# Two edits to the order of side work in a two-layer hybrid decoder kernel: a pause of the weight-sum jobs begins earlier, and two sigmoids wait for the last split of attention

## The chip, the cores and the metric

The kernel runs on one core of a Trainium2 chip. The core has a matrix engine (TensorE, PE in the profile, with PEld for its weight loads), a vector engine (VectorE, DVE), an engine for activation functions (ScalarE, ACT), a general engine (GpSimd, POOL) and a sync engine (SyncE, SP) that here only issues DMAs. Each engine works through its own queue of instructions in order; an instruction that waits for a semaphore holds up everything behind it on that engine. DMAs are issued from the queues of SP, ACT and POOL and then run by themselves.

The metric is the device time in microseconds (us) of one execution. The time of the kernel is the median over its runs.

## The reference

What is computed is a decoder trunk of two layers on 512 tokens of width 1024, all in fp32:

```python
def hybrid_layer(x, g_mix, w_in, sinks, w_a, w_b, w_out, g_mlp, w_up, w_down):
    h = rmsnorm(x, g_mix)
    z = h @ w_in
    aq, ak, av, rq, rk, rv, rg, ga, gb = jnp.split(z, SPLIT_POINTS, axis=-1)
...
    ya = sliding_window_sink_attention(aq, ak, av, sinks) @ w_a
...
    r = chunkwise_retention(rq, rk, rv)
    r = r * lax.rsqrt(jnp.mean(r * r, axis=-1, keepdims=True) + EPS)
    r = r.reshape(B, S, RET_V) * jax.nn.silu(rg.astype(jnp.float32))
    yb = r.astype(x.dtype) @ w_b
    mixed = jax.nn.sigmoid(ga) * ya + jax.nn.sigmoid(gb) * yb
    x = x + mixed @ w_out
    h2 = rmsnorm(x, g_mlp)
    x = x + jnp.square(jax.nn.relu(h2 @ w_up)) @ w_down
    return x
```

The attention looks back over 128 tokens, has 8 query heads of width 64 and a learned sink per head; the retention has 4 heads with values of width 256; the MLP is 4096 wide. A final RMS norm follows the second layer.

## The kernel before

**Precision.** Every fp32 product is made of three matmuls on rounded parts: each operand is split into a high part (a copy to the type float32r, on ACT) and a low part (the remainder, on DVE), and high times high, high times low and low times high are added in PSUM. So each block of weights that arrives from DRAM (tile `raw`, 128 partitions by 1024 numbers) costs one ACT copy (`hi`, line 342) and one DVE subtraction (`lo`, line 343) before PE may use it. Up to four blocks are split ahead of use. The same split is applied to activations by `split` (lines 417 and 418 without a scale, 420 and 421 with one).

**Fewer multiplications.** The products with the value weights, four of the retention gates, the output weights `w_wo` and the MLP weights are done in a Strassen-like form on 2 by 2 blocks with seven products instead of eight. That form needs sums of weight blocks. Where two sums share an earlier one, that earlier sum is prepared in DRAM by pairs of DMAs on POOL's queue: a plain copy of a block (line 231), and a DMA that adds a second block to it (line 234). The generator `sum_steps` (lines 216 to 245) lists these jobs for a layer, in the order of their need. For layer 0 it has one more pair at its end, for the last MLP block: a copy to `sums_last` (line 242), then two adding DMAs to it (lines 244 and 245), each of which must wait until the DMA before it has landed.

**When a job is issued.** `pace(src)` (lines 252 to 262) is called from many places where an engine has just written a tile `src`. At each second call it puts a tiny copy `mark` of one column of `src` on POOL (line 259), so that POOL waits for that tile, and behind it one step of the generator. While `quiet[0]` is true a call does nothing and isn't counted. The calls of a layer come in this order: 8 in attention, 8 from the gates of attention, 2 from the first retention query and key; then quiet; 8 from the values; 4 from the other queries and keys and 16 from the two retention pairs; 8 from the retention gates `gb`; the mixing `put_mixed` of 8 chunks; and 4 from the first half of the output product. There are none in the MLP.

**The end of the mixing stage.** x, the running activation, stays in SBUF, but from the gates of attention on its tile holds the mixed values; the true x is loaded again from DRAM. `put_mixed(c)` multiplies chunk c with its gate, adds it to `mixed[c]` (which is `x[:, c, :]`), and after odd chunks calls `first` or `second` of `Mixed`, which build the blocks for the output product; `third(0)` and `third(2)` follow after the last chunk. `third(0)` uses chunks 0, 1, 4 and 5, `third(2)` the chunks 2, 3, 6 and 7; both end in splits at lines 417 and 418. Then lines 1306 and 1307 load x again, in eight DMAs on POOL's queue, each of which may start when the splits of its chunk are done. `output()` (line 1335) multiplies with `w_wo` in seven pairs of blocks (matmuls at line 1351; each block has 24 of them) and adds the results to the reloaded x (lines 1373 and 1374).

**The end of attention.** Attention is a background task that is advanced between the chunks of the input projection. For each of four blocks of tokens, `weighted(n)` (line 753) takes its results from PSUM (lines 767 and 768) and splits them (line 769, by 417 and 418); the split of the last block is kept as `last_split`. The projection with `w_a` (lines 1189 to 1199) starts from these splits. Around it lie the sigmoid of the attention gates (line 1178), the four products `silu(i)`, i = 0 to 3, which turn the retention gates rg into rg times its sigmoid (line 1062 on ACT, 1063 on DVE), the last query and key of `qk(1)` (rotated at lines 638 to 644), and `turned.build`, which prepares blocks of the normed input for the last four retention gates (`last_gates`, matmuls at line 1015, tile `rg` in PSUM).

**What sets the order.** The framework's scheduler gives each engine its queue: it takes instructions by the order of the program, but lets a later one go ahead when by its own model of the times an earlier one is not ready. `tc.issue_after(ins)` adds an edge of order alone: what is issued in its block stands behind `ins` in the queue of the engine of `ins`. Other engines are not bound by it.

## Time and profile before

| What | Value |
|---|---|
| median of 3 runs | 1474.15 us |
| lowest and highest run | 1473.31 and 1476.63 us |
| the profiled execution | 1475.95 us |
| its span, first to last instruction | 1473.9 us |
| its mean granted TensorE clock | 0.997 |
| DMA traffic | 302.83 MB, 205 GB/s on the mean |
| DMAs from POOL's queue | 129.78 MB |

The profile was taken from one execution. Its times are microseconds from the start of the span. A row of the timeline shows start, duration, engine, line of the code, operation, the tile written and the tiles read, how many instructions are merged, and in brackets how long the engine was idle before and what ended that wait. A row of windows shows a stretch of time, then for each engine its busy time with the number of instructions, and then the granted clock of TensorE as a share of full speed, the busy share of the DMA engines and GB/s. A row of waits reads: who, for whom, total us, times, longest. The chain of waits is followed back from the last instruction, each step to what released it.

### The profile page before, as it was taken

The page shows a single profiled execution, that of the slowest core. Times are in us where ns is not written, and L with a number is a line of the kernel's source. Part 1 is how long each engine was busy: PE and PEld are TensorE (multiplying, and loading weights), DVE is VectorE, ACT ScalarE, POOL GpSimd, SP SyncE. Part 2 cuts the span into 40 slices and gives each one's busy share as a digit, 9 for nine tenths or more (in the row PEclk, how much of TensorE's full clock was granted, in tenths as well). Part 3 has the DMA queues.
Part 4 walks back from the last instruction along what each step waited for, and adds up shares of the span by engine and source line. Part 5 has one row for each costly group of instructions (what it writes and reads, how often), then busy time and mean ns, then how long its engine had stood idle before and what let it go on. Part 6 is the DMA issues. An engine that isn't in the chain of part 4 may idle for free.

```text
span 1473.9 us, 22472 instructions
## 1 busy us (share of the span) xinstructions
PE 1451.4 (98%) x8185; PEld 1271.8 (86%) x8185; DVE 1181.1 (80%) x1776; ACT 974.5 (66%) x1590; POOL 229.7 (16%) x335
## 2 busy tenths in 40 slices
PE   9999999999899999999999999999999999999998
PEld 7888888888888999999888888888889889999997
DVE  6977877868698888888779788878689888888885
ACT  6656655544487777787656576556447877777775
POOL 0011002321101111111200110022211111111120
PEclk9999999999999999999999999999999999999999
DMA  7598249999735766666964983499975477777664
GB/s 258 180 292 235 90 141 301 285 281 263 201 113 186 182 176 178 180 182 184 313 195 150 288 260 104 151 306 259 280 187 185 154 196 194 191 195 190 175 187 149
DMA packets 97295, 302.83 MB, mean 205 GB/s; under 512 B 11425, under 2 KB 11553, under 8 KB 90785
## 3 DMA queue, kind: packets, MB, share of 16 engines
q0 software_dynamic: 36512, 129.78, 37.5%
q1 hardware_dynamic: 59952, 170.32, 33.9%
q8 instruction: 64, 1.05, 0.3%
q10 hardware_dynamic: 720, 1.31, 0.2%
q14 instruction: 47, 0.38, 0.1%
HBM read 261.78 MB, written 120.06 MB: 259 GB/s over the span
## 4 chain that ended last, share of the span: by engine, by line
PE 90%; DMA 3%; issue 3%; DVE 2%; ACT 1%; POOL 1%; DVEq 0%; POOLq 0%; ACTq 0%
PE mm L395 21%; PE mm L396 21%; PE mm L394 21%; PE wo L1351 4%; PE rg L1015 3%; PE b L394 3%; PE b L395 3%; PE b L396 3%; PE rv L395 2%; PE rv L394 2%; PE rv L396 2%; PE mm L410 2%; DMA sums_up<-w_pair_in 1%; PE score L780 1%; PE pT L745 1%
## 5 line engine op out<-in xcount | busy, mean ns | idle before, releaser
L342 ACT ACTIVATE hi<-raw 128x1024 fp32r<-128x1024 f32 (+1 forms) x393 | 400.1, 1022 | 255.1 <-PE mm L395 120.0
L343 DVE TENSOR_TENSOR lo<-raw,hi 128x1024 fp32r<-128x1024 f32 (+1 forms) x394 | 458.9, 1174 | 93.7 <-ACT hi L342 90.7
L394 PE MATMUL mm<-xh,hi 128*128 128x512 f32 (+1 forms) x912 | 319.1, 354 | 1.7 <-DVE rot L642 0.6
L395 PE MATMUL mm<-xl,hi 128*128 128x512 f32 (+1 forms) x912 | 319.6, 353 | 0.0
L396 PE MATMUL mm<-xh,lo 128*128 128x512 f32 (+1 forms) x912 | 316.2, 353 | 0.1
L394 PEld LDWEIGHTS mm<-xh,hi 128*128 128x128 f32 x912 | 173.2, 190 | 25.7 <-ACT xh L420 1.3
L395 PEld LDWEIGHTS mm<-xl,hi 128*128 128x128 f32 x912 | 173.3, 190 | 21.9
L396 PEld LDWEIGHTS mm<-xh,lo 128*128 128x128 f32 x912 | 172.2, 190 | 21.5 <-DVE lo L343 0.3
L395 PE MATMUL mm<-r,hi 128*128 128x256 f32 (+1 forms) x608 | 189.3, 311 | 0.5 <-DVE r L418 0.5
L394 PE MATMUL mm<-r,hi 128*128 128x256 f32 (+1 forms) x608 | 186.2, 312 | 3.4 <-ACT r L417 2.9
L396 PE MATMUL mm<-r,lo 128*128 128x256 f32 (+1 forms) x608 | 189.0, 311 | 0.0
L394 PEld LDWEIGHTS mm<-r,hi 128*128 128x128 f32 x608 | 115.5, 190 | 12.8 <-ACT r L417 4.0
L395 PEld LDWEIGHTS mm<-r,hi 128*128 128x128 f32 x608 | 115.8, 190 | 9.4 <-DVE r L418 1.4
L396 PEld LDWEIGHTS mm<-r,lo 128*128 128x128 f32 x608 | 115.8, 190 | 6.3
L1674 POOL DMA_DIRECT2D y<-eu x56 | 63.0, 1401 | 372.0 <-DVE eu L1659 371.9
L395 PE MATMUL mm<-lo,r 128*128 128x512 f32 (+1 forms) x276 | 104.3, 387 | 0.0
L396 PE MATMUL mm<-hi,r 128*128 128x512 f32 (+1 forms) x276 | 100.9, 387 | 0.0
L394 PE MATMUL mm<-hi,r 128*128 128x512 f32 (+1 forms) x276 | 98.3, 389 | 0.3 <-ACT r L417 0.2
L394 PE MATMUL b<-hi,r 128*128 128x512 f32 x180 | 70.6, 392 | 1.9 <-DVE eu L1659 1.9
L1351 PE MATMUL wo<-r,hi 128*128 128x256 f32 x384 | 71.0, 287 | 0.0
L283 DVE TENSOR_TENSOR raw<-raw 128x512 f32<-128x512 f32 x56 | 38.5, 687 | 40.5 <-DMA raw<-w_pair_in 32.4
L395 PE MATMUL b<-lo,r 128*128 128x512 f32 x180 | 70.2, 390 | 0.0
(337 smaller groups left out, 2873.0 us busy)
## 6 DMA issues: line engine op xcount, KB each, us to landing
raw<-w_in_in SPq DMA_DIRECT2D x65, 512.0 KB, 5.5
sums_down<-w_down_in POOLq DMA_DIRECT2D x30, 1024.0 KB, 12.8
sums_up<-w_pair_in POOLq DMA_DIRECT2D x56, 512.0 KB, 12.1
raw<-w_down_in SPq DMA_DIRECT2D x45, 512.0 KB, 7.4
raw<-w_pair_in SPq DMA_DIRECT2D x84, 256.0 KB, 3.7
y<-y POOLq DMA_DIRECT2D x62, 256.0 KB, 9.7
y<-eu POOLq DMA_DIRECT2D x61, 256.0 KB, 8.5
raw<-sums_down SPq DMA_DIRECT2D x30, 512.0 KB, 7.2
```

Source lines behind the costliest of these rows:

```text
L283: nc.vector.tensor_tensor(raws[i][:, at], last[:, LEFT], last[:, RIGHT], ALU.add)
L342: state["high"] = nc.scalar.activation(hi[:, at], raw[:, at], AF.Copy).ins
L343: nc.vector.tensor_tensor(lo[:, at], raw[:, at], f32(hi[:, at]), ALU.subtract)
L394: nc.tensor.matmul(ps, ah, bh, start=start and i == 0, stop=False, **more)
L395: nc.tensor.matmul(ps, ah, bl, start=False, stop=False, **more)
L396: latest[0] = nc.tensor.matmul(ps, al, bh, start=False, stop=stop and i == n - 1, **more).ins
L410: latest[0] = nc.tensor.matmul(ps, w[:, cols(j, c)], moving[k][low], start=first, stop=bool(final)).ins
L745: nc.tensor.transpose(pt[:, i * P : (i + 1) * P], sm[:, at : at + P], ident)
L780: nc.tensor.matmul(ps[:, g * w : (g + 1) * w], q_s[g][:, c, at], part[:, keys], start=i == 0, stop=i == 1)
L1015: nc.tensor.matmul(o, w[:, cols], v, start=start and k == 0 and n == 0 and w is hi and v is vh, stop=k == 3 and n == 1 and w is lo, skip_g ...
L1351: latest[0] = nc.tensor.matmul(o, w[:, cols], v, start=start and first and n % 2 == 0 and w is hi and v is vh, stop=final and w is lo, ski ...
L1674: nc.gpsimd.dma_start(y[:, 2 * j + m, i * T : (i + 1) * T], t, **how)
```

## The change

Two places in `layer_body` change, and both hold for either layer.

```diff
         with tc.issue_after(last_exp[0]):
             for hs in (slice(0, T // 2), slice(T // 2, T)):
                 nc.scalar.activation(x[:, :, hs], x[:, :, hs], AF.Sigmoid)
-            for i in range(4):
+            for i in range(2):
+                silu(i)
+        with tc.issue_after(last_split[0]), tc.issue_after(last_split[1]):
+            for i in range(2, 4):
                 silu(i)
...
         group("w_b", layer, rT, [put_mixed(c) for c in range(4)], {1: second_pair})
+        quiet[0] = True
         for c in range(6, KD):
             gate_tile(c)
             chunk("w_in", layer, xs, gate(gates[c]))
         for c in range(4, KD):
-            quiet[0] = c > 5
             chunk("w_b", layer, rT, put_mixed(c))
         quiet[0] = False
```

The first edit: `silu(2)` and `silu(3)`, so far bound to stand behind the last exponential of attention on ACT, now stand behind the last split of attention, on ACT (the two sigmoids) and on DVE (the two products).

The second edit: the pause, which held for the calls of `put_mixed(6)` and `put_mixed(7)`, now also covers those of gates 6 and 7 and of `put_mixed(4)` and `put_mixed(5)`: four calls of `pace` per layer that no longer count. `quiet[0]` is set back to false at the same place as before, which in the program stands ahead of `third` and of the eight reloads of x; the next calls are those of `output()`.

## The prediction

> **What bounds the kernel.** I read the page first, then the waits of PE, the chain of waits, windows around the largest hole, and the queues that lead into it.

> ```profile
> span 1473.9 us, 22472 instructions
> PE 1451.4 (98%) x8185; PEld 1271.8 (86%) x8185; DVE 1181.1 (80%) x1776; ACT 974.5 (66%) x1590; POOL 229.7 (16%) x335
> PE wo L1351 <- DVE lo L343: 7.0, 1, 7.0
> PE mm L394 <- ACT r L417: 3.0, 3, 1.7
> ```

> PE is busy for 98% of the span, so time can come almost only from its holes: 1473.9 - 1451.4 = 22.5 us in all. The largest single wait, 7.0 us, is in the output product (L1351) of layer 0; the next row, at three places, is for ACT's split of activations (L417). The change touches the surroundings of both.

> ```profile
> 366.75:387.30 20.55, 20.55 (x171) 20.34 (x169) 13.21 (x17) 12.31 (x17) 5.16 (x8) 1.00 0.78 170
> 387.30:394.35 7.05, 0.00 (x1) 0.00 (x0) 1.88 (x3) 0.00 (x0) 0.00 (x0) 0.84 0.67 223
> 394.35:398.57 4.22, 4.22 (x19) 4.22 (x20) 4.22 (x6) 1.37 (x2) 1.07 (x2) 0.50 0.47 133
> ...
> 370.69 10.45 DMA sums_last<-sums_down
> 383.77 8.62 DMA x<-xT_in
> 393.08 1.23 DVE lo L343
> 394.35 14.54 PE wo L1351 x104
> ```

> The windows show PE without work for 7.05 us (387.30 to 394.35) and then 4.22 us at a granted clock of 0.50. The last four rows are the chain of waits: an adding DMA to `sums_last`, the reload of x, a weight split on DVE, PE. So a job of the weight sums, which nothing needs before the last MLP block, stands ahead of the reload that the output product needs. POOL's queue in both layers shows how:

> ```profile
> 360.02 0.83 POOL L234 DMA_DIRECT2D sums_down<-w_down_in  x1 [4.53 <-DMA sums_down<-w_down_in]
> 360.56 0.60 POOL L259 COPY mark<-gb 128x1 f32<-128x1 f32 x1
> 370.69 1.08 POOL L244 DMA_DIRECT2D sums_last<-sums_down  x1 [9.53 <-issue]
> 381.48 0.83 POOL L245 DMA_DIRECT2D sums_last<-w_down_in  x1 [9.72 <-DMA sums_last<-sums_down]
> 382.12 3.44 POOL L1307 DMA_DIRECT2D x<-xT_in  x6
> 395.28 1.07 POOL L1307 DMA_DIRECT2D x<-xT_in  x2 [9.71 <-DVE r L418]
> ...
> 1078.68 0.51 POOL L259 COPY mark<-m 128x1 f32<-128x1 f32 x1 [0.99 <-DVE m L1275]
> 1103.39 1.16 POOL L1307 DMA_DIRECT2D x<-spill  x2 [14.67 <-DVE r L418]
> 1120.17 1.06 POOL L1307 DMA_DIRECT2D x<-spill  x2 [0.58 <-DVE r L418]
> ```

> In layer 0 POOL waits 9.53 us before L244 and 9.72 us before L245; six reloads follow at once at 382.12. In layer 1 no job stands there: its last mark is at 1078.68, the reloads wait only for DVE's splits, and PE has no hole there.

> DVE's queue in layer 0:

> ```profile
> 366.79 0.68 DVE L418 TENSOR_TENSOR late<-x,late 128x512 fp32r<-128x512 f32 x1
> 378.35 1.29 DVE L418 TENSOR_TENSOR r<-x,r 128x512 fp32r<-128x512 f32 x2
> 392.47 0.69 DVE L1373 TENSOR_TENSOR x<-x,kept 128x512 f32<-128x512 f32 x1 [11.70 <-DMA x<-xT_in]
> 394.21 0.69 DVE L418 TENSOR_TENSOR r<-x,r 128x512 fp32r<-128x512 f32 x1
> ```

> DVE reaches L1373 at 380.77 (392.47 - 11.70) and stands until x lands. Behind it in the queue are the weight splits that PE lacks from 387.30 on, 6.5 us later, and the last split of `third(2)` (394.21), for which the last two reloads wait.

> **The change, part by part: the pause.** First, which jobs it moves. `pace` marks by window:

> ```profile
> 0.00:737.00 737.00, 17.44 (x29) 1.00 0.74 211
> 737.00:1473.90 736.90, 16.62 (x27) 1.00 0.70 200
> ```

> Layer 0 uses 29 steps of its generator, layer 1 27. By the order of the calls 56 have counted when the four chunks of the first mixing group are done: 28 steps. So in layer 1 all jobs are over and the earlier pause changes nothing; in layer 0 it moves one step, the 29th: the mark at 360.56 with L244 and L245. It goes to the first calls of `output()`, behind the reloads in program order. The total still suffices: 60 counted calls make 30 steps. `sums_last` is read in the last MLP block of the layer, hundreds of us later, so the step has time.

> With L244 and L245 gone from there, POOL is free at 360.85 (L234). Chunks 0, 1, 4 and 5 have their last split at 366.79 + 0.68 = 367.5, so their reloads are issued by about 368 and, with the 8.62 us of the row above, land by 377: before DVE wants the first at 380.77. The stall of DVE goes, and with it PE's 7.05 us. The slow stretch goes too: 19 matmuls took 4.22 us, where 171 in 20.55 us are 0.120 us each, or 2.28 us for 19; that is 1.94 us.

> What is late next: chunks 2 and 3, split at 378.35 + 1.29 = 379.6, reload issued by 380.7. How long it flies, from both sides:

> ```profile
> DMA to landing us min/median/max: 3.3/8.2/8.8
> DMA to landing us min/median/max: 3.4/3.6/6.2
> ```

> These are the reloads of layer 0 and of layer 1. The landing is between 384 and 389.5. The next additions that can use them need results (`kept`) that ACT had at about 386, so DVE may wait up to 3.5 us. I take nothing on PE: a stall of DVE cost PE nothing for its first 6.5 us above. If that cover were gone, it would cost the 3.5 us. Chunks 6 and 7 follow their split, now at about 383, and are wanted last. The moved step adds nothing: L244 and L245 then wait in a queue whose next user is the first MLP block, and their 1.5 MB run beside loads as they did before. Pause: -7.05 - 1.94 = -9.0 us.

> [...]

> **The two sigmoids.** The end of attention, layer 0 and then layer 1, on ACT, DVE and PE:

> ```profile
> 147.27 1.27 ACT L767 ACTIVATE whole<-pv 64x512 f32<-64x512 f32 x2 [3.71 <-PE pv L766]
> 148.57 1.15 ACT L1062 ACTIVATE sig<-z 128x512 f32<-128x512 f32 x2
> 151.94 0.61 ACT L417 ACTIVATE r<-whole 128x512 fp32r<-128x512 f32 x1
> 149.34 1.29 DVE L1063 TENSOR_TENSOR z<-z,sig 128x512 f32<-128x512 f32 x2
> 153.32 0.68 DVE L418 TENSOR_TENSOR r<-whole,r 128x512 fp32r<-128x512 f32 x1
> 152.60 1.19 PE L394 MATMUL mm<-r,hi 128*128 128x512 f32 x4 [1.21 <-ACT r L417]
> 154.06 0.50 PE L395 MATMUL mm<-r,hi 128*128 128x512 f32 x1 [0.27 <-DVE r L418]
> ...
> 882.85 1.15 ACT L1062 ACTIVATE sig<-z 128x512 f32<-128x512 f32 x2
> 886.88 1.19 PE L394 MATMUL mm<-r,hi 128*128 128x512 f32 x4 [1.65 <-ACT r L417]
> ```

> Between ACT's last read of attention (L767) and the split that PE waits for (L417) stand the two sigmoids, 1.15 us. Moved behind the split, they bring it forward by 1.15 us, inside PE's holes of 1.21 + 0.27 us and 1.65 us. DVE's two products (1.29 us) move too, so its part of the split keeps pace. I take 1.15 us in each layer, 2.3 us; the upper bound, if the scheduler also brings the split ahead of the rotation beside it, is the whole holes: 1.48 + 1.65 = 3.1 us.

> The two sigmoids and products then stand ahead of `turned.build(0)` in program order, whose work keeps its absolute time (1.15 us less before, 1.15 more behind), while PE comes 1.2 us earlier. Who waits for that is `last_gates`; the closest approach is layer 1:

> ```profile
> 910.28 0.68 DVE L418 TENSOR_TENSOR r<-xg,r 128x512 fp32r<-128x512 f32 x1
> 912.24 0.40 PE L1015 MATMUL rg<-r,hi 128*128 128x256 f32 x2
> ```

> The last split that this product needs ends at 910.96, PE begins it at 912.24 and reads that part 12 matmuls (1.4 us) later: a slack of 2.7 us, of which 1.2 us is used. Cover gone, it would cost what was gained. The retention gates 2 and 3 themselves aren't read until the retention, far behind. No table load is added: copies and sigmoids alone follow on ACT.

> **The sum.** -9.0 - 2.3 = -11.3 us. Against the profiled execution (1475.95 us: the span and 2.05 us around it) that is 1464.7 us. That execution was 1.8 us above the median 1474.15, so for a median I forecast 1463 us; with the bounds above (0 to 0.8 more from attention, scatter of the three runs) its own range is 1460 to 1466.

> **Rivals.**
> - *The second half of the reload becomes the wait* (12%). For: it is bound to the splits of `third(2)`, and chunks 2 and 3 can land as late as 389.5. Against: the 6.5 us cover, and layer 1, with the same order, without a hole. Price: 3.5 us given back: 1466.5 us. [...]
> - *The sigmoids are paid back* (10%): `build` becomes late for `last_gates` in both layers. Gain of the pause alone: 1465.2 us.
> - *The pause doesn't do what it says* (6%): my count of the calls is off by a step, or POOL is held by something else until 382. Then the sigmoids alone: 1471.9 us.
> - *Slower* (8%): the scheduler orders POOL's queue by its own times, and may put the moved step, which waits only for the second addition at L1374, ahead of the last two reloads, which wait for the last split of `third(2)`. It decides by which is ready first there. Then: PE ends the eighth block at 366.75 + 192 x 0.120 = 389.8, the mark follows at about 391.5, L244 lands 10.45 us later, L245 is issued in 0.83, the reloads land 8.62 later: 412.4, and 1.9 us on (392.47 to 394.35) PE has a split. DVE stops at about 391.5, PE 6.5 us later, at 398: a hole of 16.3 us instead of 7.05, so +9.2 - 2.3 = +6.9: 1481 us. Against it: layer 1 issued the last reloads at 1120.17, close upon the split they need, and the split precedes the additions in the program.

> **Chances and range.** Forecast 64%, the rest as above. Faster by over 0.2% (below 1471.2; less than that can't be told from no change) are the forecast and the first two rivals: 86%; within 0.2%: 6%; slower: 8%. The forecast's range is widened for reordering elsewhere by the scheduler and for the first rival: 1459 to 1469 us.

> **What would show it.** Right: in layer 0 the reloads of x stand in POOL's queue before L244 and come in pairs from about 365 to 384; DVE's wait for them at L1373 and PE's 7.0 us wait for L343 are gone; no stretch at half clock in the output product; PE's waits for L417 shrink by 1.15 us twice. Wrong: a hole of PE in that product of any other cause, a mark at `output()` ahead of reloads, or new waits of L1015 for L418.

## The result and the profile after

The changed kernel takes 1464.06 us (median of 4 runs, 1462.53 to 1464.44), beside 1474.44 us (1473.31 to 1476.63) for the kernel before on the same chip: a ratio of 0.9926 (95% interval 0.9909 to 0.9943). A later set of 4 runs gave 1462.33 us, ratio 0.9918 (0.9904 to 0.9933). The profiled execution took 1464.44 us, against 1475.95 us before.

In the changed code the lines after the first edit stand three further down: the output product is L1354, the reloads L1310, the additions L1376. The head of its page, then its waits of PE (who, for whom, total us, times, longest):

```profile
span 1462.5 us, 22466 instructions
PE 1449.4 (99%) x8185; PEld 1270.0 (87%) x8185; DVE 1182.1 (81%) x1776; ACT 974.0 (67%) x1590; POOL 226.6 (15%) x335
```

```profile
PE mm L395 <- DVE r L418: 0.8, 2, 0.4
...
PE mm L396 <- DVE lo L343: 0.5, 1, 0.5
...
PE mm L394 <- ACT r L417: 0.2, 1, 0.2
```

PE has the same work (1449.4 us) in a span that is 11.4 us shorter; its idle time fell from 22.5 to 13.1 us. The 7.0 us wait of the output product is gone, and the waits for L417 went from 3.0 to 0.2 us. The wait of 0.5 us for L343 is new.

**The pause.** POOL's queue around the output product of layer 0:

```profile
364.49 1.15 POOL L1310 DMA_DIRECT2D x<-xT_in  x2 [5.01 <-DVE r L418]
...
378.94 1.07 POOL L1310 DMA_DIRECT2D x<-xT_in  x2 [10.98 <-DVE r L418]
382.41 1.06 POOL L1310 DMA_DIRECT2D x<-xT_in  x2 [2.40 <-DVE r L418]
390.35 1.05 POOL L259 COPY mark<-x 128x1 f32<-128x1 f32 x1 [6.87 <-issue]
...
405.06 0.84 POOL L245 DMA_DIRECT2D sums_last<-w_down_in  x1 [12.60 <-DMA sums_last<-sums_down]
```

Each pair of reloads now leaves as soon as DVE has split its chunks, from 364.49 instead of 382.12 (the row left out there is the second pair, at 366.84). The moved step (the mark, then L244, left out, and L245) comes behind all eight; its 12.60 us of waiting holds nothing that PE needs. How long the reloads fly, and DVE's additions:

```profile
DMA to landing us min/median/max: 3.4/4.6/5.5
```

```profile
379.69 0.69 DVE L1376 TENSOR_TENSOR x<-x,kept 128x512 f32<-128x512 f32 x1
...
384.40 1.41 DVE L1376 TENSOR_TENSOR x<-x,kept 128x512 f32<-128x512 f32 x2
```

A row without brackets had no wait before it: DVE stands for x neither at 379.69 nor at 384.40. The whole output product of layer 0 as one window, before and after (PE, PEld, DVE, ACT, POOL, granted clock, DMA share, GB/s):

```profile
366.80:416.40 49.60, 42.39 (x337) 42.02 (x336) 36.11 (x47) 27.86 (x41) 6.23 (x10) 0.93 0.68 186
```

```profile
365.80:406.10 40.30, 40.14 (x337) 39.97 (x336) 36.50 (x47) 27.88 (x41) 6.15 (x9) 1.00 0.71 213
```

The same 337 matmuls take 40.30 us instead of 49.60: 9.3 us less. 7.05 us of that is the hole, 2.25 us the lost clock (PE busy 42.39 against 40.14). In the kernel before the clock stood at 0.50 from 392.14 to 398.97, 6.83 us, of which 2.21 us fell into the hole: that is why the prediction's window of the hole has a clock of 0.84.

**The sigmoids.** The end of attention in layer 0 on ACT, then on PE in both layers:

```profile
150.78 0.61 ACT L417 ACTIVATE r<-whole 128x512 fp32r<-128x512 f32 x1
151.30 1.14 ACT L1062 ACTIVATE sig<-z 128x512 f32<-128x512 f32 x2
152.46 0.59 ACT L638 ACTIVATE rot<-mm 64x512 f32<-64x512 f32 x1
```

```profile
151.45 0.96 PE L394 MATMUL mm<-r,hi 128*128 128x512 f32 x3
152.79 0.51 PE L395 MATMUL mm<-r,hi 128*128 128x512 f32 x1 [0.39 <-DVE r L418]
...
874.98 0.96 PE L394 MATMUL mm<-r,hi 128*128 128x512 f32 x3
876.32 0.51 PE L395 MATMUL mm<-r,hi 128*128 128x512 f32 x1 [0.38 <-DVE r L418]
```

The split (L417) stands ahead of the sigmoids and of the rotations (L638) too: the scheduler had put it behind both before. PE's holes of 1.21 and 1.65 us at L394 are gone, those at L395 grew from 0.27 to 0.39 and 0.38 us: 1.21 + 1.65 - 0.12 - 0.11 = 2.6 us. With 9.3 us that makes 11.9; the span is shorter by 11.4. What takes 0.5 us back is the new wait for L343, at 1186.55 in the MLP of layer 1; the second profile of the changed kernel doesn't have it, so it can't be put down to the change.

### The profile page after: what moved, and what is told of

It reads as the page before. It is cut to its first block, busy times and chain, and to the rows that moved or that the text cites. A ratio compares the mean times of both kernels' runs of the same rounds, so it can differ in the third digit from the quotient of the medians.

```text
span 1462.5 us, 22466 instructions
## 1 busy us (share of the span) xinstructions
PE 1449.4 (99%) x8185; PEld 1270.0 (87%) x8185; DVE 1182.1 (81%) x1776; ACT 974.0 (67%) x1590; POOL 226.6 (15%) x335
## 4 chain that ended last, share of the span: by engine, by line
PE 96%; DVE 2%; ACT 1%; DMA 1%; issue 0%; DVEq 0%
PE mm L395 22%; PE mm L394 22%; PE mm L396 22%; PE wo L1354 5%; PE rg L1015 3%; PE b L394 3%; PE b L395 3%; PE b L396 3%; PE rv L395 2%; PE rv L394 2%; PE rv L396 2%; PE mm L410 2%; PE score L780 1%; PE pT L745 1%; PE r L395 1%; PE r L396 1%
## 5 line engine op out<-in xcount | busy, mean ns | idle before, releaser
L342 ACT ACTIVATE hi<-raw 128x1024 fp32r<-128x1024 f32 (+1 forms) x393 | 400.2, 1021 | 244.9 <-PE mm L395 122.3
L343 DVE TENSOR_TENSOR lo<-raw,hi 128x1024 fp32r<-128x1024 f32 (+1 forms) x394 | 460.2, 1176 | 96.4 <-ACT hi L342 93.0
L394 PE MATMUL mm<-xh,hi 128*128 128x512 f32 (+1 forms) x912 | 319.1, 354 | 1.6 <-DVE rot L642 0.6
L395 PE MATMUL mm<-xl,hi 128*128 128x512 f32 (+1 forms) x912 | 319.6, 353 | 0.0
L394 PEld LDWEIGHTS mm<-xh,hi 128*128 128x128 f32 x912 | 173.1, 190 | 25.6 <-ACT xh L420 1.2
L395 PEld LDWEIGHTS mm<-xl,hi 128*128 128x128 f32 x912 | 173.3, 190 | 21.9
L395 PE MATMUL mm<-r,hi 128*128 128x256 f32 (+1 forms) x608 | 189.3, 311 | 0.8 <-DVE r L418 0.8
L394 PE MATMUL mm<-r,hi 128*128 128x256 f32 (+1 forms) x608 | 186.6, 312 | 0.5 <-ACT mm L1529 0.5
L394 PEld LDWEIGHTS mm<-r,hi 128*128 128x128 f32 x608 | 115.5, 190 | 9.9 <-ACT r L417 1.1
L395 PEld LDWEIGHTS mm<-r,hi 128*128 128x128 f32 x608 | 115.7, 190 | 9.6 <-DVE r L418 1.6
L395 PE MATMUL mm<-lo,r 128*128 128x512 f32 (+1 forms) x276 | 104.3, 387 | 0.0
L394 PE MATMUL mm<-hi,r 128*128 128x512 f32 (+1 forms) x276 | 98.3, 389 | 0.3 <-ACT r L417 0.2
L394 PE MATMUL b<-hi,r 128*128 128x512 f32 x180 | 70.6, 392 | 1.9 <-DVE eu L1662 1.9
L395 PE MATMUL b<-lo,r 128*128 128x512 f32 x180 | 70.2, 390 | 0.0
L1354 PE MATMUL wo<-r,hi 128*128 128x256 f32 x384 | 69.2, 283 | 0.0
```

The lines of the kernel that those rows point to most:

```text
L342: state["high"] = nc.scalar.activation(hi[:, at], raw[:, at], AF.Copy).ins
L343: nc.vector.tensor_tensor(lo[:, at], raw[:, at], f32(hi[:, at]), ALU.subtract)
L394: nc.tensor.matmul(ps, ah, bh, start=start and i == 0, stop=False, **more)
L395: nc.tensor.matmul(ps, ah, bl, start=False, stop=False, **more)
L1354: latest[0] = nc.tensor.matmul(o, w[:, cols], v, start=start and first and n % 2 == 0 and w is hi and v is vh, stop=final and w is lo, ski ...
```

## The experiments

**Each edit alone.** The first kernel is the one before with the pause alone:

```diff
         group("w_b", layer, rT, [put_mixed(c) for c in range(4)], {1: second_pair})
+        quiet[0] = True
...
-            quiet[0] = c > 5
```

> The kernel before with the earlier pause alone. My theory (the step with L244 and L245 held POOL's queue ahead of the reloads): PE's 7.0 us wait for L343 in layer 0 and the 4.2 us at half clock are gone, PE's waits for L417 at the end of attention stay at 1.21 and 1.65 us; 9.0 us less than before, about 1465.4 us. Rival (the two edits share one effect, or most of the gain comes from the sigmoids): clearly less than 9 us.

Measured: 1464.67 us beside 1475.28 us, ratio 0.9932 (0.9917 to 0.9947). Its waits of PE and its output product:

```profile
PE mm L394 <- ACT r L417: 3.0, 3, 1.7
```

```profile
366.40:406.80 40.40, 40.24 (x337) 40.03 (x337) 36.61 (x47) 27.93 (x41) 6.15 (x9) 1.00 0.70 210
```

The product falls to 40.40 us, 9.2 us less, and the end of attention keeps its waits. The second kernel has the sigmoids alone:

```diff
-            for i in range(4):
+            for i in range(2):
+                silu(i)
+        with tc.issue_after(last_split[0]), tc.issue_after(last_split[1]):
+            for i in range(2, 4):
                 silu(i)
```

> The kernel before with the moved sigmoids alone. My theory: PE's holes of 1.21 + 0.27 us and 1.65 + 0.27 us at the end of attention shrink to about 0.4 us each, as in the changed kernel; the 7.0 us hole of the output product stays; 2 to 2.7 us less than before, about 1472 us. Rival (the sigmoids are paid back at L1015, or the shift removes the hole in the output product by chance): no gain, or far more than 2.7 us.

Measured: 1471.76 us (11 runs), ratio 0.9977 (0.9968 to 0.9986), that is 3.4 us less (2.1 to 4.7). Its waits of PE:

```profile
PE wo L1354 <- DVE lo L343: 7.0, 1, 7.0
...
PE mm L394 <- ACT r L417: 0.2, 1, 0.2
```

The large wait stands as it was, the small ones are gone. From the last score product of attention to the first matmul of L1015 this trace is shorter by 1.1 us in layer 0 and 1.6 us in layer 1: 2.7 us. So both edits act, each at its place. By the ratios the two alone add to 13.4 us, where the kernel with both gained 10.9 and 12.1; the intervals of several us allow that, and the traces give 9.2 + 2.7 = 11.9.

**Does the pause act in layer 1?** The kernel before with the longer pause in layer 1 alone:

```diff
         group("w_b", layer, rT, [put_mixed(c) for c in range(4)], {1: second_pair})
+        quiet[0] = layer == 1
...
-            quiet[0] = c > 5
+            quiet[0] = layer == 1 or c > 5
```

> The kernel before with the earlier pause in layer 1 alone. My theory, by the count of the calls (27 steps used up before the gates 6 and 7 of layer 1): no job moves, the time is that of before within 0.2%, the 7.0 us hole of layer 0 stays. Rival (the pause helps wherever it stands, by less work on POOL): some us less.

Measured: 1474.94 us, ratio 1.0001 (0.9992 to 1.001). The hole of layer 0 stays:

```profile
PE wo L1352 <- DVE lo L343: 6.7, 1, 6.7
```

The whole gain of the pause is in layer 0, as the count of the generator's steps had it.

**Waiting or traffic?** The moved step did two things at its old place: POOL stood still, and its DMAs moved 1.5 MB beside the loads. Two kernels part these, both from the changed one. The first moves bytes without a wait: 2 MB of plain copies in layer 0, half of them ahead of the reloads, half between them, and the reloads sorted so that chunks 0, 1, 4 and 5 come first.

```diff
+        if layer == 0:
+            mark = small.tile([P, 1], F32, tag="mark", name="mark", bufs=2)
+            ins = nc.gpsimd.tensor_copy(mark, gates[7][:, 0:1])
+            with tc.issue_after(ins.ins):
+                extra = dram.tile([P, 4 * UNIT], F32, name="extra")
+                nc.gpsimd.dma_start(extra[:, : 2 * UNIT], w_down[0, N_BLOCK - 1][:, : 2 * UNIT])
...
-        for c in range(KD):
-            nc.gpsimd.dma_start(x[:, c, :], source[:, c, :])
+        for c in (0, 1, 4, 5, 2, 3, 6, 7):
+            ins = nc.gpsimd.dma_start(x[:, c, :], source[:, c, :])
+            if layer == 0 and c == 5:
+                with tc.issue_after(ins.ins):
+                    nc.gpsimd.dma_start(extra[:, 2 * UNIT :], w_down[0, N_BLOCK - 1][:, 2 * UNIT :])
```

> The changed kernel with two further plain copies of 1 MB in DRAM on POOL's queue in layer 0, which wait for no earlier DMA: one where L244 stood before (behind a mark on gate 7), one between the fourth and the fifth reload. So the traffic of the moved step is back, and more, but not its waiting. My theory (what cost time was that L244 and L245 hold POOL's queue until the DMA before them lands): the reloads are issued from about 365 to 384 as in the changed kernel, they land up to some us later, DVE may wait up to 3 us, PE at most 1 us; the time is that of the changed kernel within 0.2%. Rival (the reload was slow because the DMA engines were full with the step's data): a hole of PE of several us in the output product, up to the 9 us of before.

Measured: 1461.33 us, ratio 0.991 (0.9895 to 0.9925). A window from just before the reloads, with the second copy in it:

```profile
360.00:390.00 30.00, 30.00 (x238) 29.34 (x237) 28.09 (x34) 16.58 (x23) 6.67 (x11) 1.00 0.80 276
```

At 276 GB/s, more than in either kernel's output product, PE is busy for all 30.00 us. The copies don't stand directly ahead of the reloads in time: the first was issued 8 us before them. The second kernel waits and moves almost nothing: eight copies of 8 KB, each dependent on the one before, stand ahead of the reloads of layer 0.

```diff
+                hops = dram.tile([8, P, 16], F32, name="hops")
+                nc.gpsimd.dma_start(hops[0], w_down[0, N_BLOCK - 1][:, :16])
+                for k in range(7):
+                    hop = nc.gpsimd.dma_start(hops[k + 1], hops[k])
...
+        with tc.issue_after(hop.ins) if layer == 0 else ExitStack():
+            for c in range(KD):
+                nc.gpsimd.dma_start(x[:, c, :], source[:, c, :])
```

> The changed kernel with a chain of eight tiny DMAs (8 KB each) on POOL's queue in layer 0, where L244 stood before; each reads what the one before wrote, so each waits until that has landed, and the reloads stand behind the chain. The waiting of the moved step is back without its traffic. At 2 to 3 us for each (the 64 KB copies of this kernel land in 2.0 us, the smallest on POOL's queue in 2.6) POOL is held to between 376 and 385, against 382 before. My theory: the reloads land 3 to 6 us behind that, DVE stands at its first addition to x for some us, and PE has a hole in the output product whose length follows the end of the chain: none if POOL is free by 374, 1 to 4 us at 378, 5 us and more at 382, with some us at half clock behind a long one. Rival (traffic): no hole, 1464 us.

Measured: 1471.89 us (10 runs, 1468.39 to 1474.22), ratio 0.9979 (0.9969 to 0.9989). POOL's queue, DVE's, and the window of the hole:

```profile
365.43 0.51 POOL L1307 DMA_DIRECT2D hops<-hops  x1 [10.69 <-DMA hops<-w_down_in]
...
379.33 0.49 POOL L1307 DMA_DIRECT2D hops<-hops  x1 [1.66 <-DMA hops<-hops]
380.12 3.21 POOL L1319 DMA_DIRECT2D x<-xT_in  x6 [0.31 <-issue]
```

```profile
387.01 0.69 DVE L1385 TENSOR_TENSOR x<-x,kept 128x512 f32<-128x512 f32 x1 [9.33 <-DMA x<-xT_in]
```

```profile
384.00:388.89 4.89, 0.21 (x2) 0.01 (x1) 1.88 (x3) 0.00 (x0) 0.00 (x0) 0.84 0.49 156
```

The picture of the kernel before is back at 156 GB/s: six reloads at once at 380.12, DVE idle for x, PE empty, and half clock (here from 387.34 to 394.16). So the waiting in POOL's queue is enough for a hole. It doesn't give the whole of it: the hole is 4.7 us (4.89 - 0.21) and not 7.05, and this execution (1469.34 us) is among the shorter of its ten. The cover shows too: DVE stops at 377.68 (387.01 - 9.33), PE runs dry at 384.21, 6.5 us later, as in the kernel before.

What is missing is in the flight of the reloads. These are the six at 380.12:

```profile
DMA to landing us min/median/max: 3.2/4.5/5.4
```

In the kernel before the same six took 7.8 to 8.8 us. There they were issued 0.6 us and more behind L245, which landed at 388.45, and the first of them landed at 389.96. The reload that DVE waits for is the fourth: 8.62 us in the kernel before, 5.14 here. Without these 3.5 us the hole of 7.05 us would have been about 3.6, an estimate from these rows; here POOL issued the first reload 2.44 us after DVE's stop and in the kernel before 1.35, and with the difference of 1.1 us that makes the 4.7 us that were measured. So the moved step cost time in two ways: it held POOL's queue, and the reloads that then left right behind its last DMA landed only after that. The second made about half of the hole. Whether the reloads were held by their place in the queue or by the transfer ahead taking the DMA engines, no run separates. The plain copies of the kernel with traffic alone, each issued 8 us or more ahead of the next reload, don't test it; the reloads there took up to 6.5 us.

**How much lateness is free?** The changed kernel with half of the step back at its old place: L244 as its own step, for which gates 6 and 7 count again, and L245 behind the reloads.

```diff
             nc.gpsimd.dma_start(sums_last, s1.unsqueeze(1).broadcast_to([P, 2, UNIT]), accum_op=ALU.add)
+            yield
             nc.gpsimd.dma_start(sums_last[:, 1, :], r12, accum_op=ALU.add)
...
-        quiet[0] = True
         for c in range(6, KD):
             gate_tile(c)
             chunk("w_in", layer, xs, gate(gates[c]))
         for c in range(4, KD):
+            quiet[0] = True
             chunk("w_b", layer, rT, put_mixed(c))
```

> The changed kernel with the moved step cut in two: L244 back at gate 7, ahead of the reloads, L245 still behind them. POOL then waits for L244's inputs until about 370 and can issue the first four reloads from about 371 to 374. My theory (DVE has until 380 before it wants x, and then 6.5 us of cover on PE): they land by about 381, PE has no hole in the output product, the time is that of the changed kernel, 1464 us, within 0.2%. Rival (every us by which the reloads are late costs PE a us): 5 to 7 us more, since the first reloads come that much later than at 364 to 368.

Measured: 1463.28 us, ratio 0.9924 (0.991 to 0.9937). Its lines stand one further down than in the changed kernel. POOL, the flight of the four reloads, DVE and PE:

```profile
369.70 1.07 POOL L244 DMA_DIRECT2D sums_last<-sums_down  x1 [9.98 <-issue]
370.29 2.69 POOL L1311 DMA_DIRECT2D x<-xT_in  x4
```

```profile
DMA to landing us min/median/max: 10.3/12.0/12.2
```

```profile
384.32 0.69 DVE L1377 TENSOR_TENSOR x<-x,kept 128x512 f32<-128x512 f32 x1 [4.25 <-DMA x<-xT_in]
```

```profile
401.58 0.47 PE L1355 MATMUL wo<-late,hi 128*128 128x256 f32 x2 [0.99 <-DVE x L1378]
```

The reloads were expected by about 381 and landed at 384.20: they had left right behind L244, which landed at 379.95, and took 10.3 to 12.2 us where the changed kernel's took 3.4 to 5.5. It is the same flight behind an earlier DMA as above. The stall of DVE of 4.25 us cost PE no weight split. It cost 0.99 us elsewhere, at a block where the changed kernel waits for 0.16 us: the additions of DVE (L1378) had fallen behind, and the last block waited for the result they were to take out of PSUM. The runs can't tell that from the changed kernel.

**The rival on the slower side, made to happen.** The changed kernel with the reloads of chunks 6 and 7 bound behind the moved step:

```diff
-            nc.gpsimd.dma_start(sums_last[:, 1, :], r12, accum_op=ALU.add)
+            state["job"] = nc.gpsimd.dma_start(sums_last[:, 1, :], r12, accum_op=ALU.add).ins
...
-        for c in range(KD):
+        for c in range(KD if layer else 6):
             nc.gpsimd.dma_start(x[:, c, :], source[:, c, :])
...
+                    if layer == 0 and (i, j, m) == (0, 0, 1):
+                        with tc.issue_after(state["job"]):
+                            for c in (6, 7):
+                                nc.gpsimd.dma_start(x[:, c, :], source[:, c, :])
```

> The changed kernel with the moved step (its mark at the second addition of the output product, L244, L245) ahead of the reloads of chunks 6 and 7: the order that the rival 'slower' of the prediction names. Its price there was 16.3 us of hole instead of none, so about 16 us plus half-clock time over the changed kernel: 1481 us. What speaks for less: the scheduler knows of the later reload and may put work of DVE ahead of the addition that needs it, and PE reads chunks 4 to 7 of x last; then 5 to 12 us more, 1469 to 1476 us. If nothing is lost (1464 us), the place of the moved step does not matter and the rival was no danger.

Measured: 1477.55 us (10 runs), ratio 1.0015 (1.0006 to 1.0025). POOL, DVE, and the windows at the hole:

```profile
404.52 1.33 POOL L1389 DMA_DIRECT2D x<-xT_in  x2
```

```profile
412.46 0.69 DVE L1376 TENSOR_TENSOR x<-x,kept 128x512 f32<-128x512 f32 x1 [7.87 <-DMA x<-xT_in]
```

```profile
405.19:414.34 9.15, 0.00 (x1) 0.00 (x1) 1.88 (x3) 3.55 (x8) 0.67 (x2) 0.72 0.59 115
414.34:420.00 5.66, 5.66 (x14) 4.52 (x15) 5.66 (x11) 0.91 (x2) 0.00 (x0) 0.54 0.51 185
```

It eats the whole gain: 15.2 us over the changed kernel run beside it (1477.55 - 1462.33). L245 leaves at 403.88, after 12.10 us of waiting for L244, and the reloads behind it land at about 412, as the rival had it, but the hole is 9.15 us and not 16.3: meanwhile the scheduler had put other work of the next stage ahead, so DVE stops only at 404.59 (412.46 - 7.87). PE follows 0.6 us later, at 405.19, in the first MLP product. The cover of 6.5 us belongs to the output product; here it was 0.6. The hole and about 2.6 us of half clock make 11.8 us. Between the two traces, 14.6 us apart, another 1.5 us were there ahead of the edit already (the last score product of layer 0 starts at 124.8 and 123.3); the rest I have not traced.

**What does a sigmoid ahead of the split cost?** The kernel before, with the sigmoids of gates 2 and 3 computed twice into the same tile:

```diff
             s = temp("sig")
+            if i in (2, 3):
+                nc.scalar.activation(s, rg[i], AF.Sigmoid)
             nc.scalar.activation(s, rg[i], AF.Sigmoid)
```

> The kernel before with the sigmoids of retention gates 2 and 3 computed twice (two more ACT instructions per layer at the place where they stood before the change). My theory (each us of ACT ahead of the last split is a us of PE at the end of attention): PE's holes for L417 grow from 1.21 and 1.65 us by 1.15 us each, to about 2.4 and 2.8 us; about 2.3 us more than before, 1477 us. Rival (PE's hole there is set by something else, such as DVE's half of the split): no growth, 1474.6 us.

Measured: 1481.4 us beside 1474.83 us, ratio 1.0047 (1.0034 to 1.0061): 6.9 us, far more than expected. PE's rows of both layers, then windows at the holes, with edges where the trace has a change of the clock or could have one:

```profile
151.62 2.08 PE L394 MATMUL mm<-r,hi 128*128 128x512 f32 x4 [2.24 <-ACT r L417]
...
889.64 1.19 PE L394 MATMUL mm<-r,hi 128*128 128x512 f32 x4 [2.69 <-ACT r L417]
891.87 0.59 PE L395 MATMUL mm<-r,hi 128*128 128x512 f32 x1 [1.04 <-DVE r L418]
```

```profile
148.03:151.44 3.41, 1.35 (x7) 0.90 (x5) 2.48 (x5) 3.37 (x6) 0.00 (x0) 1.00 0.00 0
151.44:158.27 6.83, 6.50 (x14) 4.63 (x15) 6.04 (x10) 5.02 (x9) 0.56 (x1) 0.50 0.48 156
...
885.31:888.72 3.41, 1.64 (x8) 1.11 (x6) 1.75 (x4) 3.35 (x6) 0.00 (x0) 1.00 0.01 2
888.72:892.13 3.41, 1.45 (x5) 0.94 (x6) 3.15 (x6) 3.39 (x7) 0.00 (x0) 1.00 0.15 37
892.13:895.55 3.42, 3.42 (x9) 2.65 (x9) 2.89 (x5) 2.08 (x4) 0.56 (x1) 0.50 0.76 267
```

The holes at L394 grew by 1.03 and 1.04 us, as the 1.15 us of sigmoids lets expect. That at L395 in layer 1 grew by 0.77 us. The rest is the clock: PE worked 6.50 us and 3.42 us at 0.50, which makes about 5.0 us lost. Together that is 7.8 us, within the interval of 5.0 to 9.0.

When the clock fell can be read from these windows. In this trace it changed at 151.44, 158.27, 892.13 and 895.55, in that of the kernel before at 392.14, 398.97 and 1470.75: within each trace whole multiples of 3.41 us apart (151.44 to 892.13 are 217 of them, 392.14 to 1470.75 are 316). So each of these traces shows a grid of windows of that length. In each of the three falls at holes the clock came back behind the first window in which PE was never idle, at 158.27, 895.55 and 398.97. Here the hole of 2.24 us lies nearly whole in one window: 3.41 - 1.35 = 2.06 us idle, 60%. The longer hole of 2.69 us is cut by an edge at 888.72. Its first part left 1.77 us idle, 52%, and the clock stayed; its second part and the hole of 1.04 us made 1.96 us, 57%, and the clock fell. In the kernel before the window ahead of the fall, 388.73 to 392.14, was idle throughout; behind one with 48% (883.66 to 887.07, at its hole of 1.65 us) the clock stayed.

A smaller dose, then: the kernel before with the sigmoid of gate 2 alone doubled.

```diff
+            if i == 2:
+                nc.scalar.activation(s, rg[i], AF.Sigmoid)
             nc.scalar.activation(s, rg[i], AF.Sigmoid)
```

> The kernel before with the sigmoid of retention gate 2 alone computed twice: 0.57 us more of ACT ahead of the last split in each layer, half of what the doubling of two gave (6.6 us more, with PE's holes at 2.24 us and at 2.69 + 1.04 us, and about 6 and 3.5 us at half clock behind them). Theory: the holes grow by 0.57 us each, to 1.8 us and 2.2 us, and the large price of the doubling came from the half clock, which holes of this size need not bring: 1.1 us more than before, 1476 us, if the clock stays full at both; 2 to 3 us more for each layer in which it falls. Rival (the price is in proportion to the work added, by some other path): 3.3 us more, with full clock.

Measured: 1476.94 us (12 runs, 1475.27 to 1480.07) beside 1475.0 us, ratio 1.0017 (1.0008 to 1.0025), 2.5 us. Two windows of the grid at the holes of layer 1 in its profiled execution, then PE's rows of both layers, and DVE's in layer 0:

```profile
882.26:885.67 3.41, 1.61 (x8) 1.11 (x6) 2.46 (x4) 3.35 (x6) 0.00 (x0) 1.00 0.01 2
885.67:889.09 3.42, 2.10 (x8) 1.45 (x9) 3.08 (x5) 3.38 (x7) 0.41 (x1) 1.00 0.14 46
```

```profile
151.07 1.19 PE L394 MATMUL mm<-r,hi 128*128 128x512 f32 x4 [1.73 <-ACT r L417]
153.22 0.50 PE L395 MATMUL mm<-r,hi 128*128 128x512 f32 x1 [0.96 <-DVE r L418]
...
886.04 1.19 PE L394 MATMUL mm<-r,hi 128*128 128x512 f32 x4 [2.17 <-ACT r L417]
888.19 0.50 PE L395 MATMUL mm<-r,hi 128*128 128x512 f32 x1 [0.95 <-DVE r L418]
```

```profile
150.74 0.68 DVE L644 TENSOR_TENSOR rot<-rot,rot 128x512 f32<-128x512 f32 x1
...
152.48 0.69 DVE L418 TENSOR_TENSOR r<-whole,r 128x512 fp32r<-128x512 f32 x1
```

The clock stayed at 1.00 at the holes of both layers: an edge cuts the hole of 2.17 us, and the window with the most idle time has 1.80 us, 53%. So what these holes cost here is not the clock's. The holes at L394 grew by 0.52 us, the time of one sigmoid; those at L395 by 0.69 and 0.68 us, because the scheduler now put the last rotation (L644, 0.68 us) ahead of DVE's split. In the kernel before, the split began at 153.32 and the rotation behind it, at 153.92.

0.52 + 0.69 + 0.52 + 0.68 = 2.4 us, and by the ratio the runs show 2.5 (1.2 to 3.7). The profiled execution is no longer than that of the kernel before (1475.63 against 1475.95 us), mainly because it was 2.1 us ahead at the last score product of layer 0, ahead of the edit. Where the edges of the grid fall differs from execution to execution: in the two profiles of the kernel before the clock fell 4.84 and 5.18 us into the same hole. So the clock may have fallen in the executions near 1480 us; no trace of one shows it.

**Is there cover behind the split?** The changed kernel with the sigmoids of gates 2 and 3 doubled:

```diff
+            if i in (2, 3):
+                nc.scalar.activation(s, rg[i], AF.Sigmoid)
             nc.scalar.activation(s, rg[i], AF.Sigmoid)
```

> The changed kernel with the same doubling, so that the added 1.15 us of ACT per layer stands behind the last split and ahead of the blocks for the last retention gates. My theory (2.7 us of slack there, 1.2 of it used): no new wait of L1015, the time is that of the changed kernel, 1463 us, within 0.2%. Rival (the sigmoids are paid back at the last gates): PE waits at L1015 for L418 or L417, 1 to 2 us more.

Measured: 1464.88 us, ratio 0.9934 (0.9921 to 0.9948). The 6.9 us are not there. From the last score product to the end of the last gates (L1015) the trace is about 1.3 us longer in each layer than that of the changed kernel. No product of L1015 waits for L418. A new wait comes in each layer instead; layer 0's row:

```profile
184.61 0.73 PE L394 MATMUL rv<-hi,xh 128*128 128x512 f32 x2 [1.03 <-ACT hi L342]
```

It is ACT's weight split that is late, and the scheduler has put the first product of the retention values ahead of one of L1015. So the end of attention is free of the added sigmoids, but behind it PE waited 1.03 us in each layer where 1.15 us of work were added, and not at the place that the prediction named. The scheduler's new order is mixed into this number, so it doesn't tell how much of the added work was covered, nor does it measure the slack.

**The kernels again.** The changed one, run again:

> The changed kernel once more, beside the next three on one chip. 1464 us; no hole of PE in the output product of layer 0.

Measured: 1462.33 us, as told above. And the kernel before against itself:

> The kernel before once more, for a second profile: whether the granted clock stays full at its holes of 1.21 + 0.27 us and 1.65 + 0.27 us. By the first profile it does, and the time is that of before, 1474.8 us.

Measured: ratio 0.9998 (0.9988 to 1.0008), with the holes of the first profile at the end of attention and a wait of 6.6 us for L343. Differences of about 0.1% are thus the floor of these comparisons. None of these versions clearly beats the changed kernel; 1461.33 us with 2 MB of extra copies lies within the interval of the kernel that it was made from.

## Why the prediction was right

The forecast was 1464.7 us for a profiled execution and 1463 for a median; 1464.44 us and medians of 1464.06 and 1462.33 were measured. The mechanism was right at both places; that the profiled execution was met within 0.3 us is in part luck, since both terms were 0.3 us too small, a new wait of 0.5 us took most of that back, and executions of the changed kernel lie up to 4 us apart.

- *What bounds the kernel.* Right. PE's work did not change, and the time came out of its holes and of the slow stretch behind one.
- *Which jobs the pause moves.* Right: one step in layer 0, none in layer 1. The pause in layer 1 alone changed nothing.
- *The pause, -9.0 us.* Right: -9.3 in the product of the changed kernel, -9.2 alone. The term for the clock, 1.94 us, counted the 19 matmuls of a window that ended at 398.57; the half clock lasted until 398.97, and PE's busy time in the whole product fell by 2.25.
- *Why the step cost that.* Right, but not all of it. The prediction saw POOL's queue held; a wait without traffic brings back a hole of 4.7 us. The other part it had in its rows and didn't name: the reloads that left right behind L245 flew 7.8 to 8.8 us. It counted with 8.62 us for the first reloads of the changed kernel too and with up to 8.8 for the next, where they took 3.4 to 5.5, so its landing times were on the safe side.
- *The second half of the reload.* The risk was smaller than the prediction held: the reloads of chunks 2 and 3, issued from 378.94 on, landed at 382.42 and 383.50, and DVE's addition to them began at 384.40. Where the reload was made late, a stall of 4.25 us cost 0.99 us, so the 3.5 us of that rival were too high: the weight splits were covered, the additions were not.
- *The sigmoids, -2.3 us.* Right in the mechanism, 0.3 us too small: 2.6 us. The prediction held the rotation to be in front of the split still; the scheduler brought the split ahead of it, the case that the upper bound of 3.1 us named. That bound, which left out the 0.27 us of layer 1, wasn't reached since DVE's half of the split became the last wait, by 0.39 and 0.38 us. No table load came in: ACT has 17 in either trace, 1.28 us each, and none between 147 and 160 us.
- *Cover behind the split.* Enough for the change. With more work there PE waited for ACT's L342 and not, as the prediction had it, L1015 for L418; how much cover was left is open.
- *The slower rival.* It did not happen by itself: the mark came at 390.35, 7 us after the last reloads. Forced, it made the kernel slower than before by 2.2 us (0.9 to 3.7); its price of 6.9 was too high, as the hole moved into the MLP.

## What to carry to other kernels

A queue served in order passes a wait on to everything behind it (here POOL's 9.72 us ahead of L245 to six reloads), and here transfers that left right behind a large one landed only after that (from 389.96 on, behind 388.45): look for a job that waits for its own earlier DMA and stands ahead of a transfer with a near need, and move the job that nobody needs yet, not the transfer. When a chain on one engine is late, ask how much prepared work the engine behind it still has, at that very place: the same kind of stall was free for 6.5 us in one product and for 0.6 us in the next. A short operation ahead of the one that PE waits for was paid in full here, and two or three times over where it changed the scheduler's order or dropped the clock (1.1 us of sigmoids cost 2.5 us, 2.3 us cost 6.9). Whether a hole dropped the clock depended here on how it lay in the grid of windows, which the trace shows, and not on its length alone: it fell behind a hole of 2.24 us that lay nearly whole in one window, and stayed at one of 2.17 us that an edge cut.
